# Layer 0's probabilities times values for all key blocks of a group in one piece, and the output weights' last split ahead of the first gated sum

## The chip, the cores and the metric

The kernel runs on one core of one Trainium2 chip. The core has five engines that each take their instructions in the order in which the program holds them: TensorE (PE, matmuls; PEld is its weight load), VectorE (DVE), ScalarE (ACT), GpSimd (POOL), and SyncE (SP), which here issues the DMAs. An engine whose next instruction waits for another engine or for a DMA stands still, and everything behind that instruction stands with it. The metric is the device time of one execution in microseconds (us). Before the change three runs gave a median of 1699.66 us (1698.5 to 1700.81).

## What is computed

Two layers of a diffusion backbone over 512 latent tokens and 256 context tokens of width 1024. Layer 0 mixes tokens by windowed attention with 16 query heads and 2 key/value heads of 64 and a sink logit per head; layer 1 by differential attention. Each layer goes on with a squared-ReLU MLP of width 4096. Sums pass through LayerNorm with DeepNorm scaling and gates from a conditioning vector. All is in float32.

```python
def block_fn(args):                       # layer 0, for each block of 128 queries
    s_lat = jnp.where(valid, einsum('bqhgd,bkhd->bhgqk', qblk, kblk) * scale, NEG_INF)
    s_ctx = einsum('bqhgd,bchd->bhgqc', qblk, kc) * scale
    p = softmax_with_sink(jnp.concatenate([s_lat, s_ctx], axis=-1), sink_f)
    o = einsum('bhgqk,bkhd->bqhgd', p[..., :3 * BLOCK], vblk)
    return o + einsum('bhgqc,bchd->bqhgd', p[..., 3 * BLOCK:], vc)
...
x = layer_norm(alpha * x + g1 * ax, ln1_g[i], ln1_b[i])     # ax = attention output @ wo
fx = sqrelu_mlp(x * (1.0 + sc2) + sh2, mlp_w1[i], mlp_w2[i])
x = layer_norm(alpha * x + g2 * fx, ln2_g[i], ln2_b[i])
```

## The kernel before

Tokens stand in six blocks of 128 (`tb`): four latent, two context. A weight of 128x1024 is loaded by DMA to `w_raw`, rounded by ACT to `w_h` (L264) and its remainder taken by DVE as `w_l` (L260); a product is then three matmuls, `w_h` times both parts of the tokens and `w_l` times one (`mm3`, L318 to L320). `wsplit` makes such a weight. Three raw buffers and four pairs of split buffers go round.

**What sets the order.** PE's order is fixed when the program is built. Generator jobs yield the conditions under which they can go on; a planner (`Flow`) keeps an estimated clock for every engine, and at each point lets the job of the smallest priority number go on whose condition holds. It knows a price per instruction by its size, and none for what stands next to it. For the other engines a scheduler orders the instructions by its own estimates, within dependences that the kernel can add by hand (`tc.add_manual_dep` with `ORDER`: the first instruction is to stand behind the second in the queue, without a semaphore).

**Layer 0's attention** works in 24 groups, each one block of queries and four heads (`group`). Groups of the four latent query blocks see 4 or 5 key blocks (two, or two or three, latent ones beside two of context), and the eight groups of the context blocks see 2. For each of the four heads PE makes the scores `s_ps` (two slots), DVE takes mask and minimum (`nm`), ACT the exponential `e` with its sum, DVE the reciprocal, POOL the product. Then for each key block `i` four transposes on PE put the probabilities of the four heads side by side in `pT_ps`; ACT (even `i`) or DVE (odd `i`) copies them to a buffer `pT`; and `av` multiplies them by the values `vv` into `o_ps`, two matmuls (128 rows by 64 columns of the array: even heads to the upper 64 partitions of the output, odd heads to the lower). `pend` is the list of the blocks that are copied and not multiplied yet, `pS` counts the `pT` buffers, four of them. `av` runs for two blocks as soon as both copies are due, or for the last one alone.

Jobs of larger priority numbers fill in: the query projection `q_ps`, then the streamed modulation weights (`ada_ps`, 12 pieces of eight matmuls that use 32 columns of the array each, and `ada_t`, their transposes), and from the end of those on the first half of the output projection (`out_proj`: `y_ps` with weights `a_wo`, six matmuls a piece). The projection of a token block can start once all four groups of that block are done.

**Layer 1's output projection** begins before its attention ends: for seven of the eight products of a token block and a half of the columns, three of the four weights (`u` = 0 to 2) are multiplied early (`out1`). The fourth weight of the second half (`st2["W1"]`) is split in `mlp1`'s first lines; `main1` then finishes the products in the order (half 0, block 0), (half 1, block 0), (half 0, block 1) and so on, and `gated_add` multiplies each with the gate (`g_tmp`) and adds it to `acc`; `stats` follows, then the LayerNorm.

Of the kernel before, what the change touches and what calls it, by code (L numbers as in the profile page):

```python
# [19 lines left out]
P = 128  # L20
D = 1024
# [195 lines left out]
def pool2(n):  # L217
    return n * 0.0022 + 0.12
# [16 lines left out]
def hybrid_block(ctx: ExitStack, tc: tile.TileContext, t: dict, out: bass.AP):  # L235
# [23 lines left out]
    def dv(n, deps, fn, lat=LAT, **kw):  # L259
        fn(**kw)  # L260
        return fl.op("D", dve(n), deps, lat)
# [5 lines left out]
    def gp(us, deps, fn, lat=LAT, **kw):  # L267
        fn(**kw)  # L268
        return fl.op("G", us, deps, lat)
# [29 lines left out]
    def wsplit(src, n=1024, raw=None, hl=None, pool=False):  # L299
        if raw is None:  # L300
            raw = raw_tile()
        if hl is None:
            hl = [wpool.tile([P, 1024], F32R, name="w_" + x, tag="w" + x, bufs=NH) for x in "hl"] + [rwh.get(), rwh]
        raw, rg, rr = raw
        h, l, hg, hr = hl
        q = dma(n, [rg], out=raw[:, :n], in_=src)
        a = ac(n, [q, hg], nc.scalar.copy, out=h[:, :n], in_=raw[:, :n])
        kw = dict(out=l[:, :n], in0=raw[:, :n], in1=f(h)[:, :n], op=ALU.subtract)
        d = gp(pool2(n), [a], nc.gpsimd.tensor_tensor, **kw) if pool else dv(n, [a], nc.vector.tensor_tensor, **kw)
        d.ring = rr  # L310
        rel = Task()
        rel.ring = hr
        return Weight(h, l, d, rel)
# [242 lines left out]
    def gated_add(pool, give, acc, half, pt, p, gate, last, scale=1.0):  # L556
        cs_ = slice(half * 512, (half + 1) * 512)
        tm = pool.tile([P, 512], F32, name="g_tmp", tag="tmp", bufs=2)
        m = dv(512, [p], nc.vector.tensor_tensor, out=tm, in0=pt, in1=gate[:, cs_], op=ALU.mult)
        give(m)  # L560
        if scale != 1.0:
            return dv(512, [m], nc.vector.scalar_tensor_tensor, out=acc[:, cs_], in0=acc[:, cs_], scalar=scale, in1=tm,
                      op0=ALU.mult, op1=ALU.add)
        if last:
            return dv(512, [m], nc.vector.tensor_tensor, out=acc[:, cs_], in0=acc[:, cs_], in1=tm, op=ALU.add)
        return gp(pool2(512), [m], nc.gpsimd.tensor_tensor, out=acc[:, cs_], in0=acc[:, cs_], in1=tm, op=ALU.add)
# [170 lines left out]
    with tc.tile_pool(name="qpool", bufs=6, side="right") as qpool, \  # L737
# [219 lines left out]

        oT = hx
        eS = Slots(fl, EB)
        pS = Slots(fl, 4)  # L960

        def etile(i):
            if i < EB:
# [3 lines left out]
        def group(n, tb, qd):  # L967
# [61 lines left out]


            def av_ok():
                return (len(pend) > 1 or len(pend) == 1 and i == len(kbs)) and fl.ok([x[3] for x in pend[:2]])


            i = 0
            while i < len(kbs) or pend:
                yield lambda: (YES if (i < len(kbs) and fl.ok([sm_.ok, pS.ok])) or av_ok() else NO)
                if i < len(kbs) and fl.ok([sm_.ok, pS.ok]) and len(pend) < 4:
                    pp = psm("pT_ps")
                    slot = sm_.take()  # L1040
                    for c, j in enumerate((0, 2, 1, 3)):
                        nc.tensor.transpose(out=pp[:, c * P:(c + 1) * P], in_=es[j][:, i * P:(i + 1) * P],  # L1042
                                            identity=ident)
                    p = fl.pe(4 * mm(128))
                    pt_ = pool.tile([P, 512], F32, name="pT", tag="pT", bufs=4)
                    xi = pS.take()
                    r = (dv(512, [p], nc.vector.tensor_copy, lat=XLAT, out=pt_, in_=pp) if i % 2 else
                         ac(512, [p], nc.scalar.copy, lat=XLAT, out=pt_, in_=pp))
                    sm_.give(slot, r)
                    if i == len(kbs) - 1:  # L1050
                        for q_ in esl:
                            eS.give(q_, p)
                    pend.append((i, kbs[i], pt_, r, xi))
                    i += 1
                else:
                    for _ in range(min(2, len(pend))):
                        p = av(*pend.pop(0))
            st0["done"] += 1
            if st0["done"] % 4 == 0:
# [468 lines left out]
    with tc.tile_pool(name="mlp1", bufs=1, reuse_waits="tile") as pool:  # L1528
        xraw["pool"] = pool
        hl = [late.tile([P, 1024], F32R, name="w_" + x, tag="w" + x, bufs=1) for x in "hl"]  # L1530
        acc = [pool.tile([P, D], F32, name="acc1", tag="acc", bufs=NXB) for _ in range(NXB)]
        for tb in range(NXB):
            dma(D, [], out=acc[tb], in_=x_res[tb])
        gx = bcast_load(pool, gate_d[(1, 2)][0:1], "g1x")
        queue["behind"] = queue["last"]
        st2["W1"].append(wsplit(t["b_wo"][1, 3], hl=hl + [None, None]))
        lb = bcast_load(pool, lnrow[1, 1:2], "l1b")
        scale_inplace(lb, ALPHA)
        A, B = affine(1, 0, 1, 1, 3, 4, "m1", 1)
        hx = hx_big("hx1m", SEQ)  # L1540
        ready = [NO] * NXB

        def done3(tb, st, r):
            fl.add(ln_job(pool, acc[tb], tb, hx, A, B, ready, st, r), 0)

        def done4(tb, st, r):
            if tb == 0:
                st2["g"] = bcast_load(pool, lnrow[1, 2:3], "l2g")
                st2["b"] = bcast_load(pool, lnrow[1, 3:4], "l2b")
            mv, rstd, d = moments(st, r)  # L1550
            cols = [slice(0, D)] if tb < NXB - 1 else [slice(0, 512), slice(512, D)]
            for c in cols:
                dv(c.stop - c.start, [r], nc.vector.scalar_tensor_tensor, out=acc[tb][:, c], in0=acc[tb][:, c],
                   scalar=mv[:, 0:1], in1=st2["g"][:, c], op0=ALU.subtract, op1=ALU.mult)
            for c in cols:
                dv(c.stop - c.start, [d], nc.vector.scalar_tensor_tensor, out=acc[tb][:, c], in0=acc[tb][:, c],
                   scalar=rstd, in1=st2["b"][:, c], op0=ALU.mult, op1=ALU.add)
                nc.sync.dma_start(out=out[tb * P:(tb + 1) * P, c], in_=acc[tb][:, c])

        def g2b():  # L1560
            yield
            return [bcast_load(pool, gate_d[(1, 5)][0:1], "g2x")]

        def main1():
            yield from tok_product(pool, oT, {0: st2["W"], 1: st2["W1"]}, [(h_, tb) for tb in range(NXB) for h_ in range(2)],
                                   acc, (gx,), done3, pre=st2["po"], late=(0, 1))
            queue["behind"] = None
            reload(gx, lnrow[1, 0:1])
            scale_inplace(gx, ALPHA)
            res = [lambda tb=tb: residual(acc[tb], gx, lb, last["pe"]) for tb in range(NXB)]  # L1570
            yield from mlp(1, hx, ready, apool, pool, SEQ, acc, g2b, done4, None, res)

        fl.add(main1(), 2)
        fl.run()
# [71 lines left out]
```

## Time and profile before

| | |
|---|---|
| median of three runs | 1699.66 us (1698.5 to 1700.81) |
| the profiled execution | 1701.68 us, its span 1699.9 us, mean granted clock 0.988 |
| layer 0's attention, scores to last group | about 70 to 323 us of the span |
| layer 1's output projection | about 1280 to 1327 us |

The page gives busy times by engine, the chain of work that ended last, and groups of instructions; the trace behind it gives single rows. A row of the timeline holds the start in us from the span's start, how long it took from its first instruction's start to its last one's end, the engine, line, operation, `out<-in`, the form, how many instructions are merged in it, and in square brackets how long the engine stood idle ahead of it and what ended that. Matmuls overlap, so their price is read from one start to the next. A product of plain float32 appears as two records, so `av` of one block as four. A stretch shows busy times of all engines between two points; its clock (1.00, or 0.50 in a few stretches) is what the throttle granted PE.

### The profile page before, as it was taken

The numbers are of one execution on the slowest core, as the hardware profiler recorded it, in microseconds if no ns is written. First come the engines' busy times: TensorE is split into PE (matmuls) and PEld (weight loads), VectorE is DVE, ScalarE is ACT, GpSimd is POOL, SyncE is SP. The second block draws the span as 40 slices with busy tenths as digits, with TensorE's granted clock in tenths as the row PEclk, the third lists the DMA queues.
The fourth block names the chain that finished last, engine by engine and source line by source line (L and its number), as shares of the span: only waits on it lengthen the run. The fifth ranks groups of instructions, "written<-read, shape, count | busy, mean of one in ns | idle before, by whom it ended". The sixth has DMA issues, their size and how long they took to land.

```text
span 1699.9 us, 23452 instructions
## 1 busy us (share of the span) xinstructions
PE 1626.4 (96%) x9129; PEld 1394.2 (82%) x9129; DVE 955.2 (56%) x1811; ACT 657.8 (39%) x1281; POOL 346.6 (20%) x314
## 2 busy tenths in 40 slices
PE   6899899999999999999999999999989799999998
PEld 4787567789879989979978998999877788888886
DVE  3665677676855444444446777677655553233436
ACT  3455565362223213202316555555542533222230
POOL 1234444200001101243220223221100001103422
PEclk9999999999999999999999999999899899999999
DMA  9110343343535334334323122211132323132321
GB/s 363 41 50 8 125 153 109 127 152 108 166 116 168 113 124 136 112 111 137 99 66 112 50 69 67 69 44 38 47 111 100 103 73 134 63 124 75 111 87 50
DMA packets 57240, 174.78 MB, mean 103 GB/s; under 512 B 7144, under 2 KB 13096, under 8 KB 57128
## 3 DMA queue, kind: packets, MB, share of 16 engines
q1 hardware_dynamic: 57128, 173.27, 30.6%
q8 instruction: 72, 1.18, 0.3%
q14 instruction: 40, 0.33, 0.1%
HBM read 165.35 MB, written 7.90 MB: 102 GB/s over the span
## 4 chain that ended last, share of the span: by engine, by line
PE 75%; DVE 10%; issue 5%; ACT 5%; DMA 3%; POOL 3%; SPq 0%; DVEq 0%; POOLq 0%; ACTq 0%
PE y_ps L320 10%; PE y_ps L319 10%; PE y_ps L318 10%; PE h_ps L318 8%; PE h_ps L319 8%; PE h_ps L320 8%; PE qkv_ps L318 2%; PE qkv_ps L319 2%; PE qkv_ps L320 2%; PE s_ps L1340 2%; PE o_ps L1024 2%; DVE w_l L260 2%; DVE e L260 2%; PE pT_ps L1042 2%; PE o_ps L1378 1%
## 5 line engine op out<-in xcount | busy, mean ns | idle before, releaser
L264 ACT CAST w_h<-w_raw 128x1024 fp32r<-128x1024 f32 (+1 forms) x185 | 186.4, 1015 | 414.6 <-PE y_ps L320 210.9
L260 DVE TENSOR_TENSOR w_l<-w_raw,w_h 128x1024 fp32r<-128x1024 f32 (+1 forms) x185 | 221.8, 1210 | 220.1 <-ACT w_h L264 219.2
L319 PE MATMUL y_ps<-w_l,hid 128*128 128x512 f32 x640 | 253.0, 395 | 1.8 <-DVE w_l L260 1.7
L320 PE MATMUL y_ps<-w_h,hid 128*128 128x512 f32 x640 | 253.0, 395 | 0.4 <-DVE hid L260 0.2
L318 PE MATMUL y_ps<-w_h,hid 128*128 128x512 f32 x640 | 253.1, 395 | 0.0
L268 POOL TENSOR_TENSOR relu<-relu 128x768 f32<-128x768 f32 (+1 forms) x48 | 80.7, 1681 | 609.4 <-ACT relu L264 609.4
L320 PE MATMUL h_ps<-hx0m,w_l 128*128 128x384 f32 (+1 forms) x528 | 176.2, 334 | 1.6 <-DVE w_l L260 1.6
L318 PE MATMUL h_ps<-hx0m,w_h 128*128 128x384 f32 (+1 forms) x528 | 176.3, 334 | 0.2 <-ACT w_h L264 0.2
L319 PE MATMUL h_ps<-hx0m,w_h 128*128 128x384 f32 (+1 forms) x528 | 175.8, 333 | 0.0
L319 PEld LDWEIGHTS y_ps<-w_l,hid 128*128 128x128 f32 x640 | 120.4, 188 | 31.3 <-DVE w_l L260 3.1
L320 PEld LDWEIGHTS y_ps<-w_h,hid 128*128 128x128 f32 x640 | 120.3, 188 | 30.0 <-DVE hid L260 1.6
L318 PEld LDWEIGHTS y_ps<-w_h,hid 128*128 128x128 f32 x640 | 120.4, 188 | 28.4
L318 PE MATMUL qkv_ps<-w_h,hx 128*128 128x384 f32 (+1 forms) x384 | 127.8, 333 | 0.1
L319 PE MATMUL qkv_ps<-w_l,hx 128*128 128x384 f32 (+1 forms) x384 | 123.3, 321 | 0.8 <-DVE w_l L260 0.8
L320 PE MATMUL qkv_ps<-w_h,hx 128*128 128x384 f32 (+1 forms) x384 | 123.2, 321 | 0.0
L268 POOL TENSOR_TENSOR e<-e,sm 128x512 f32<-128x512 f32 (+2 forms) x96 | 94.3, 998 | 120.4 <-DVE sm L260 79.8
L318 PE MATMUL h_ps<-hx1m,w_h 128*128 128x512 f32 (+1 forms) x288 | 107.8, 374 | 3.5 <-ACT relu L264 3.5
L319 PE MATMUL h_ps<-hx1m,w_h 128*128 128x512 f32 (+1 forms) x288 | 107.4, 373 | 0.0
L320 PE MATMUL h_ps<-hx1m,w_l 128*128 128x512 f32 (+1 forms) x288 | 107.3, 373 | 0.0
L320 PEld LDWEIGHTS h_ps<-hx0m,w_l 128*128 128x128 f32 x528 | 99.6, 189 | 2.9 <-DVE w_l L260 2.9
L318 PEld LDWEIGHTS h_ps<-hx0m,w_h 128*128 128x128 f32 x528 | 99.7, 189 | 0.8 <-ACT w_h L264 0.6
L319 PEld LDWEIGHTS h_ps<-hx0m,w_h 128*128 128x128 f32 x528 | 99.7, 189 | 0.1
(225 smaller groups left out, 3118.3 us busy)
## 6 DMA issues: line engine op xcount, KB each, us to landing
w_raw<-in_w SPq DMA_DIRECT2D x128, 512.0 KB, 3.5
w_raw<-in_w_adaT SPq DMA_DIRECT2D x56, 512.0 KB, 3.5
w_raw<-in_w_ada SPq DMA_DIRECT2D x24, 512.0 KB, 4.3
w_raw<-in_b_w SPq DMA_DIRECT2D x32, 384.0 KB, 3.2
raw<-in_w_ada SPq DMA_DIRECT2D x16, 512.0 KB, 9.7
w_raw<-in_a_wq SPq DMA_DIRECT2D x8, 512.0 KB, 4.4
w_raw<-in_a_wo SPq DMA_DIRECT2D x8, 512.0 KB, 4.3
w_raw<-in_b_wo SPq DMA_DIRECT2D x8, 512.0 KB, 3.6
```

The source lines that it names most:

```text
L260: fn(**kw)
L264: fn(**kw)
L268: fn(**kw)
L318: nc.tensor.matmul(out=o, lhsT=lh, rhs=rh, start=start, stop=False)
L319: nc.tensor.matmul(out=o, lhsT=lh, rhs=rl, start=False, stop=False)
L320: last["pe"] = nc.tensor.matmul(out=o, lhsT=ll, rhs=rh, start=False, stop=stop)
L1024: nc.tensor.matmul(out=po[odd * HD:odd * HD + HD, 0:256], lhsT=vv[:, kb, kvh], rhs=pt_[:, odd * 256:odd * 256 + 256], start=(i == 0), stop ...
L1042: nc.tensor.transpose(out=pp[:, c * P:(c + 1) * P], in_=es[j][:, i * P:(i + 1) * P], identity=ident)
L1340: nc.tensor.matmul(out=sp[:, c * 512:c * 512 + 384], lhsT=qTt[:, tt, hl, qb * P:(qb + 1) * P], rhs=kS[:, tt, c * 384:c * 384 + 384], start ...
L1378: nc.tensor.matmul(out=po[:, qp * 256:(qp + 1) * 256], lhsT=vt[:, kb, vl], rhs=pt_[:, pl, a * 256:a * 256 + 256], start=(kp == 0 and pl == ...
```

## The change

Three edits. In `group` there are six `pT` buffers in place of four, and `av` runs only when all blocks of the group are transposed and copied, or when no buffer is left; then for all that are pending. In `wsplit` the DVE's subtraction is kept by name, and `gated_add` orders its first multiplication behind the one that `mlp1` names: the split of the output weights' last part. No instruction is added or removed.

```diff
@@ wsplit
-        d = gp(pool2(n), [a], nc.gpsimd.tensor_tensor, **kw) if pool else dv(n, [a], nc.vector.tensor_tensor, **kw)
+        if pool:
+            d = gp(pool2(n), [a], nc.gpsimd.tensor_tensor, **kw)
+        else:
+            last["split"] = nc.vector.tensor_tensor(**kw)
+            d = fl.op("D", dve(n), [a])
@@ gated_add
-        m = dv(512, [p], nc.vector.tensor_tensor, out=tm, in0=pt, in1=gate[:, cs_], op=ALU.mult)
+        i = nc.vector.tensor_tensor(out=tm, in0=pt, in1=gate[:, cs_], op=ALU.mult)
+        if queue.get("split"):
+            tc.add_manual_dep(i.ins, queue.pop("split"), ORDER, reason="queue order")
+        m = fl.op("D", dve(512), [p])
@@ layer 0, group
-        pS = Slots(fl, 4)
+        pS = Slots(fl, 6)
...
-                return (len(pend) > 1 or len(pend) == 1 and i == len(kbs)) and fl.ok([x[3] for x in pend[:2]])
+                return pend and (i == len(kbs) or not fl.ok(pS.ok)) and fl.ok([x[3] for x in pend])
...
-                if i < len(kbs) and fl.ok([sm_.ok, pS.ok]) and len(pend) < 4:
+                if i < len(kbs) and fl.ok([sm_.ok, pS.ok]):
...
-                    pt_ = pool.tile([P, 512], F32, name="pT", tag="pT", bufs=4)
+                    pt_ = pool.tile([P, 512], F32, name="pT", tag="pT", bufs=6)
...
-                    for _ in range(min(2, len(pend))):
+                    for _ in range(len(pend)):
                         p = av(*pend.pop(0))
@@ mlp1
         st2["W1"].append(wsplit(t["b_wo"][1, 3], hl=hl + [None, None]))
+        queue["split"] = last["split"].ins.name
```

Three places of the order follow; the lines' numbers shift by up to eight. On PE, the sixth group (five key blocks) before, from its first `av` (`o_ps`, x4 is two blocks) on; `e_1488`, `e_1527`, `e_1508` and `e_1607` are its four heads' probabilities:

```order
L1024 MATMUL o_ps<-pT,v_118 64x256 x4
L1042 MATMUL pT_ps<-identr,e_1488 128x128
L1042 MATMUL pT_ps<-identr,e_1527 128x128
L1042 MATMUL pT_ps<-identr,e_1508 128x128
L1042 MATMUL pT_ps<-identr,e_1607 128x128
L1024 MATMUL o_ps<-pT,v_118 64x256 x4
L987 MATMUL s_ps<-kT_117,qT_1307 128x384 x2
L991 MATMUL s_ps<-kT_117,qT_1307 128x256 x2
L1024 MATMUL o_ps<-pT,v_118 64x256 x2
```

The same group after the change, from the transposes of its last key block on:

```order
L1049 MATMUL pT_ps<-identr,e_1545 128x128
L1049 MATMUL pT_ps<-identr,e_1583 128x128
L1049 MATMUL pT_ps<-identr,e_1564 128x128
L1049 MATMUL pT_ps<-identr,e_1662 128x128
L364 MATMUL ada_ps<-w_raw,cs 32x256 x8
L994 MATMUL s_ps<-kT_117,qT_1292 128x384 x2
L998 MATMUL s_ps<-kT_117,qT_1292 128x256 x2
L994 MATMUL s_ps<-kT_117,qT_1292 128x384 x2
L998 MATMUL s_ps<-kT_117,qT_1292 128x256 x2
L1031 MATMUL o_ps<-pT,v_118 64x256 x10
L388 MATMUL ada_t<-identr,ada_rows 128x128 x2
```

Three pieces of two, two and one blocks became one of five, and an `ada_ps` piece and two heads' scores of a later group stand between the last transposes and it. On PE, the end of the stage before: the last head's scores, and what stands ahead of the last group's transposes (after these rows come two more of `y_ps` and then the transposes):

```order
L991 MATMUL s_ps<-kT_117,qT_1841 128x256 x2
L318 MATMUL y_ps<-w_h,hx_92 128x512
L319 MATMUL y_ps<-w_l,hx_92 128x512
L320 MATMUL y_ps<-w_h,hx_92 128x512
L318 MATMUL y_ps<-w_h,hx_92 128x512
L319 MATMUL y_ps<-w_l,hx_92 128x512
L320 MATMUL y_ps<-w_h,hx_92 128x512
L1024 MATMUL o_ps<-pT,v_118 64x256 x4
L318 MATMUL y_ps<-w_h,hx_93 128x512
L319 MATMUL y_ps<-w_l,hx_93 128x512
L320 MATMUL y_ps<-w_h,hx_93 128x512
L318 MATMUL y_ps<-w_h,hx_93 128x512
```

The same place after the change; `e_3625` is the head whose scores stand in the first row:

```order
L998 MATMUL s_ps<-kT_117,qT_1791 128x256 x2
L1031 MATMUL o_ps<-pT,v_118 64x256 x4
L1049 MATMUL pT_ps<-identr,e_3551 128x128
L1049 MATMUL pT_ps<-identr,e_3585 128x128
L1049 MATMUL pT_ps<-identr,e_3574 128x128
L1049 MATMUL pT_ps<-identr,e_3625 128x128
```

Behind them come the second block's four transposes and the group's `av`. The `y_ps` pieces that stood here now stand earlier in the stage: the first one comes after the `av` of 11 groups, where it came in the midst of the fifteenth group's before. On DVE, at layer 1's output projection before:

```order
L260 TENSOR_TENSOR oT_8245<-oraw,oT_8245 128x512 x2
L260 TENSOR_TENSOR g_tmp<-y_ps,g1x 128x512
L260 TENSOR_TENSOR acc_12405<-acc_12405,g_tmp 128x512
L260 BN_STATS bn<-acc_12405 128x6
L260 TENSOR_TENSOR w_l<-w_raw,w_h 128x1024
L260 TENSOR_SCALAR l1b<-l1b 128x1024
L260 TENSOR_TENSOR g_tmp<-y_ps,g1x 128x512
```

And after the change:

```order
L260 TENSOR_TENSOR oT_8245<-oraw,oT_8245 128x512 x2
L312 TENSOR_TENSOR w_l<-w_raw,w_h 128x1024
L260 TENSOR_SCALAR l1b<-l1b 128x1024
L563 TENSOR_TENSOR g_tmp<-y_ps,g1x 128x512
L260 TENSOR_TENSOR acc_12405<-acc_12405,g_tmp 128x512
L260 BN_STATS bn<-acc_12405 128x6
L563 TENSOR_TENSOR g_tmp<-y_ps,g1x 128x512
```

The split moved ahead of the first gated sum, and the scaling of `l1b` with it; nothing else on DVE moved there. SP's queue holds the same DMAs; in layer 0 the loads of the modulation weights and of `a_wo` stand earlier in the program, and two small loads of the gate (`g1h`) stand ahead of the last modulation weight and the first of `a_wo`, where they stood behind the first of `a_wo`.

## The prediction

> **What bounds the kernel now.** I read the page first (busy shares, then the chain that ended last), then the stretches of the layer-0 attention, then who TensorE (PE) waits for in them.
>
> ```profile
> span 1699.9 us, 23452 instructions
> ...
> PE 1626.4 (96%) x9129; PEld 1394.2 (82%) x9129; DVE 955.2 (56%) x1811; ACT 657.8 (39%) x1281; POOL 346.6 (20%) x314
> ...
> PE 75%; DVE 10%; issue 5%; ACT 5%; DMA 3%; POOL 3%; SPq 0%; DVEq 0%; POOLq 0%; ACTq 0%
> ```
>
> PE is busy 96% of the span and holds 75% of the chain, so time is won in two ways only: PE does its work in less time, or one of its waits goes. The stretches (from:to, length, then busy us of PE, PEld, DVE, ACT, POOL, then clock, DMA share, GB/s) say the same of the attention:
>
> ```profile
> 180.00:260.00 80.00, 71.96 (x623) 49.29 (x624) 53.80 (x178) 44.73 (x106) 36.82 (x32) 1.00 0.47 152
> 325.00:345.00 20.00, 20.00 (x88) 16.10 (x87) 12.53 (x19) 3.17 (x4) 1.11 (x2) 1.00 0.85 288
> ```
>
> In the attention (first row) no other engine is full, and DMA is at 0.47; in the output projection behind it (second row) PE has no gap at all. PE's waits between 100 and 330 us (total, times, longest):
>
> ```profile
> PE s_ps L987 <- DVE nm L260: 3.6, 6, 2.2
> PE o_ps L1024 <- ACT pT L264: 2.2, 2, 1.4
> PE ada_t L384 <- ACT ada_rows L264: 1.6, 1, 1.6
> PE ada_ps L360 <- DMA w_raw<-in_w_ada: 1.1, 1, 1.1
> PE o_ps L1024 <- DVE pT L260: 0.6, 1, 0.6
> ```
>
> **Part 1: the AV matmuls in one pack.** Nothing is computed that was not computed before: 88 key blocks (16 latent groups of 4 or 5, eight context groups of 2), four AV records each. The order makes 47 packs of AV matmuls before and 24 after. What one pack costs beside its blocks is read from packs of one, two and three blocks (x4, x8, x12):
>
> ```profile
> 159.13 0.65 PE L1024 MATMUL o_ps<-pT,v 128*64 128x256 f32 x4
> 159.71 0.62 PE L987 MATMUL s_ps<-kT,qT 128*128 128x384 f32 x2
> ...
> 226.99 1.52 PE L1024 MATMUL o_ps<-pT,v 128*64 128x256 f32 x12
> 228.43 1.07 PE L360 MATMUL ada_ps<-w_raw,cs 128*32 128x256 f32 x16
> ...
> 279.76 0.39 PE L319 MATMUL y_ps<-w_l,hx 128*128 128x512 f32 x1
> 279.99 0.39 PE L320 MATMUL y_ps<-w_h,hx 128*128 128x512 f32 x1
> 280.31 1.08 PE L1024 MATMUL o_ps<-pT,v 128*64 128x256 f32 x8
> 281.33 0.74 PE L991 MATMUL s_ps<-kT,qT 128*128 128x256 f32 x4
> ```
>
> From start to the next row's start they take 0.58, 1.02 and 1.44 us: 0.43 us a block and 0.15 fixed. The pack also starts 0.32 us after the y_ps row ahead of it, where y_ps rows follow each other after 0.23: 0.09 more. So a pack costs 0.24 us beside its work, wherever the array goes from 128*128 to 128*64 and back. 23 packs fewer: 23 x 0.24 = 5.5 us. Eight times before, and once after, a pack stands next to an ada_ps row (128*32), which starts a pack of its own kind; there the two share one change, 7 x 0.09 = 0.6 us that is lost. Net **-4.9 us** of PE work in a stretch where PE is the bound.
>
> **The waits of that stretch.** The order is drawn anew, so each wait is looked up in it.
>
> The 2.8 us of o_ps waiting for its pT copies (ACT 2.2, DVE 0.6): before, a pack began as soon as two copies were due. Now at least one pair of score matmuls, and mostly an ada_ps or y_ps piece, stands between a five-block group's last transposes and its pack, and the last block is asked for 4 x 0.43 = 1.7 us into the pack. Bounds 0 and -2.8; I take **-2.7**. The two ada waits (1.6 and 1.1): now the pack of 2.3 us stands between an ada_ps piece and its ada_t, and ada_ps pieces are 3.5 us apart or more. Bounds 0 and -2.7; I take **-2.4**. The other s_ps waits (3.6 less 2.2, 1.4 us) stay, and grow because PE comes 5 us earlier to a DVE that has the same work: between 0 and as much again; **+0.7**.
>
> The longest wait, 2.18 us, has a cause of its own (chain row, DVE row, PE row, two stretches, and the loads' median time to landing):
>
> ```profile
> 249.90 6.18 DMA w_raw<-in_a_wo
> ...
> 257.18 1.23 DVE L260 TENSOR_TENSOR w_l<-w_raw,w_h 128x1024 fp32r<-128x1024 f32 x1 [2.49 <-ACT w_h L264]
> ...
> 259.46 0.51 PE L987 MATMUL s_ps<-kT,qT 128*128 128x256 f32 x2 [2.18 <-DVE nm L260]
> ...
> 256.85:260.26 3.41, 1.23 (x10) 0.99 (x9) 3.08 (x10) 1.17 (x4) 0.00 (x0) 1.00 0.84 282
> 260.26:263.67 3.41, 3.41 (x18) 3.19 (x18) 2.42 (x9) 3.41 (x8) 1.36 (x2) 0.50 0.34 136
> ...
> w_raw<-in_a_wo SPq DMA_DIRECT2D x8, 512.0 KB, 4.3
> ```
>
> The first output weights land 6.18 us after their issue, ACT and DVE stand in order behind them, and PE's scores behind DVE. Right behind it PE runs 3.41 us at half clock: 1.7 us lost. After the change these four splits come some 16 us of PE work earlier, and the first to ask for the late ones is y_ps itself: from the release of the second load PE has 6.2 us of rows until it needs that weight's low part. Load, cast and split take 4.3 to 6.2 (median and longest load) + 1.05 + 1.23 = 6.6 to 8.5 us, so PE waits 0.4 to 2.3 us. Two gate loads that ran beside the slow load are now issued ahead of the last w_ada load, so I take the short side, 0.8: **-1.4**, and half of the clock loss: **-0.85**.
>
> **What is late next: the end of the stage.** Because the output projection starts earlier, its y_ps rows are used up before the last group. There the order has: last score matmul, a pack of two blocks, the group's transposes, its pack, nothing between. How long a head's chain is, shows at the same place before:
>
> ```profile
> 314.58 0.48 PE L991 MATMUL s_ps<-kT,qT 128*128 128x256 f32 x2
> 315.62 0.47 DVE L260 CUSTOM_DVE_ANT_0 e<-s_ps,mask,nsink 128x256 f32<-128x256 f32 x1
> 316.57 0.51 ACT L264 ACTIVATE e<-e,nm 128x257 f32<-128x257 f32 x1 [0.57 <-DVE e L260]
> 317.44 0.61 POOL L268 TENSOR_TENSOR e<-e,sm 128x256 f32<-128x256 f32 x1 [0.41 <-DVE sm L260]
> 318.89 1.03 PE L1042 MATMUL pT_ps<-identr,e 128*128 128x128 f32 x8
> 319.52 0.59 ACT L264 COPY pT<-pT_ps 128x512 f32<-128x512 f32 x1 [1.64 <-PE pT_ps L1042]
> 319.96 0.69 DVE L260 COPY pT<-pT_ps 128x512 f32<-128x512 f32 x1 [1.62 <-PE pT_ps L1042]
> ```
>
> From the scores' end (315.06) to POOL's end (318.05) 3.0 us. The last group's fourth transpose has only a pack of two (1.1) and three transposes (0.35) to hide it: 1.6 us idle. Its copies end 1.22 and 1.76 us after the first transpose, where PE's eight take 0.87: about 0.55 more. **+2.2 us**. Bounds 0 (a chain half as long) and 3.0.
>
> The clock may add to that. The row above shows that a stretch of 3.41 us with PE at work for 1.23 was followed by one at half clock, and the tail has 2.2 us of waits and 1.7 of transposes close together: another 1.7 us, at even odds **+0.85**. [...]
>
> Layer 0 together: -4.9 - 2.7 - 2.4 + 0.7 - 1.4 - 0.85 + 2.2 + 0.85 = **-8.5 us**. Behind it PE is busy 20.00 of 20 us (325:345 above), so what is won there is kept.
>
> **Part 2: the last split ahead of the first gated sum.**
>
> ```profile
> 1290.95 1.04 ACT L264 CAST w_h<-w_raw 128x1024 fp32r<-128x1024 f32 x1
> ...
> 1299.41 0.69 DVE L260 TENSOR_TENSOR g_tmp<-y_ps,g1x 128x512 f32<-128x512 f32 x1 [7.63 <-PE y_ps L320]
> ...
> 1301.46 1.21 DVE L260 TENSOR_TENSOR w_l<-w_raw,w_h 128x1024 fp32r<-128x1024 f32 x1
> 1302.59 0.69 DVE L260 TENSOR_SCALAR l1b<-l1b 128x1024 f32<-128x1024 f32 x1
> ...
> 1302.73 0.50 PE L319 MATMUL y_ps<-w_l,oT 128*128 128x512 f32 x1 [3.13 <-DVE w_l L260]
> 1304.18 0.69 DVE L260 TENSOR_TENSOR g_tmp<-y_ps,g1x 128x512 f32<-128x512 f32 x1 [0.91 <-PE y_ps L320]
> ...
> 1304.18:1322.63 18.45, 15.49 (x78) 12.40 (x76) 18.23 (x37) 9.35 (x20) 1.64 (x3) 0.98 0.29 112
> ...
> 1283.52 0.43 SPq L275 DMA_DIRECT2D l1b<-in_lnrow  x1
> DMA to landing us min/median/max: 5.0/5.0/5.0
> ```
>
> The split's input is ready at 1291.99, and DVE idles 7.63 us until the first y_ps is done. Put ahead, it runs from 1292.0 to 1293.2 in that idle time, and the scaling of l1b (landed by 1288.5), which moves with it, to 1293.9. The added order has g_tmp wait for an instruction that ended 5 us earlier: nothing. PE's wait of 3.13 us goes. The next limit is DVE: it is busy 18.23 of the following 18.45 us. Its second g_tmp moves from 1304.18 to the end of the first sum's statistics at 1301.46; PE, resuming at 1299.6, has that product by 1301.1. **-2.7 us**, bounds -2.2 and -3.13. The raw buffer comes free 9 us earlier and its next load with it; the cast behind that load waits for PE, so nothing collides.
>
> **The sum.** -8.5 - 2.7 = -11.2 us against the profiled execution's 1701.68: 1690.5. That execution lies 2.0 us over the median of the three runs; against 1699.66 the sum gives 1688.5. A redrawn order also has small waits that I did not find; what I did not list before (0.2 to 0.4 us each) suggests some 1.5 us. Forecast: **1690.0 us**.
>
> **The rivals.**
> - *The tail and the weights eat layer 0's gain.* If y_ps waits 2.3 us for its weights and halves the clock as before, the tail halves it too (+1.7), the ada waits only move and half of the o_ps waits stays, layer 0 is at -4.9 - 1.4 + 0.1 + 0.7 + 2.2 + 1.7 = -1.6, with part 2 at -4.3, with the small waits at -2.8: 1696.9, inside 0.2%. For it: both places stand in the order. Against: it needs each bound at its bad end. 0.15.
> - *Slower: half clock in the groups.* [...] 0.05.
> - *Part 2 gives nothing*, if the first sum was to wait anyway: 1692.7. DVE's 7.63 idle us speak against it. 0.08.
> - That the packs don't form is excluded by the order: 24, one a group.
>
> **How the numbers follow.** Forecast 0.72. Half-clock windows elsewhere can come or go as the work shifts, 1.7 us each; two fewer and an open tail at 0 give 1684.5, the first rival 1697: the range. A measurement here tells about 0.2% (3.4 us) from no change; faster by more 0.82 (forecast, most of the third rival and a part of the first), within 0.14, slower 0.04.
>
> **What would show it.** Right: PE's o_ps packs in 24 pieces with 0.24 us saved a pack; no o_ps wait over 0.5 us before the last group; PE idle near 1.6 us ahead of the last transposes; no y_ps wait of 3.13 us, DVE's gap ahead of g_tmp at about 5.7 us. Wrong: a wait over 3 us in the attention that before has not, or half-clock stretches in it.

## The result and the profile after

| | before | after |
|---|---|---|
| median of 7 runs each | 1698.5 us (1692.58 to 1700.81) | 1685.71 us (1683.57 to 1690.51) |
| ratio, 95% interval | | 0.9938 (0.9921 to 0.9955) |
| the profiled execution, its span | 1701.68 us, 1699.9 us | 1690.51 us, 1688.7 us |
| layer 0's first transposes to the next stage's first, on PE | 244.01 us | 238.15 us |

The change makes the kernel faster by 0.45 to 0.79%. The ratio is taken over all executions and is not the quotient of the two medians, which is 0.9925. One execution of a run reported below, the kernel before with later copies, took 1799.99 us at a granted clock of 0.846, where its other seven had 0.988 to 0.993, and is left out of that row. The three lines of the page after that answer to those of before:

```profile
span 1688.7 us, 23443 instructions
...
PE 1617.0 (96%) x9129; PEld 1392.0 (82%) x9129; DVE 956.7 (57%) x1811; ACT 658.2 (39%) x1281; POOL 344.4 (20%) x314
...
PE 74%; DVE 10%; issue 5%; ACT 4%; DMA 3%; POOL 3%; SPq 0%; POOLq 0%; DVEq 0%; ACTq 0%
```

PE executes the same 9129 records, 9.4 us less busy time; shares and chain look the same. Where the time went shows only by stretch. The stage of the table, before and after (from:to, length, then busy us of PE, PEld, DVE, ACT, POOL, then clock, DMA share, GB/s):

```profile
102.09:346.10 244.01, 234.57 (x1608) 174.95 (x1607) 164.34 (x513) 120.50 (x285) 94.32 (x96) 0.99 0.31 100
```

```profile
101.61:339.76 238.15, 228.22 (x1609) 175.11 (x1608) 163.35 (x512) 120.97 (x285) 94.10 (x96) 0.99 0.31 102
```

PE is busy 234.57 - 228.22 = 6.35 us less in it, while its idle time (length less busy) goes from 9.44 to 9.93. So the whole gain of the first part is in PE's work and none is in its waits, although the waits are different ones. PE's waits after, between 100 and 330 us (total, times, longest):

```profile
PE pT_ps L1049 <- ACT pT L264: 2.9, 4, 0.9
PE pT_ps L1049 <- POOL e L268: 2.2, 1, 2.2
PE y_ps L323 <- DVE w_l L312: 1.5, 2, 1.3
PE ada_t L388 <- ACT ada_rows L264: 1.4, 2, 0.8
PE o_ps L1031 <- DVE pT L260: 0.9, 2, 0.6
PE ada_ps L364 <- DMA w_raw<-in_w_ada: 0.6, 1, 0.6
PE o_ps L1031 <- ACT pT L264: 0.2, 1, 0.2
PE s_ps L994 <- DVE nm L260: 0.2, 1, 0.2
```

The s_ps waits of 3.6 us are down to 0.2, the o_ps waits from 2.8 to 1.1; in their place transposes wait (pT_ps, 5.1 us). What the largest group of these is, the records around one of them show (start, length, engine, line, operation, and in brackets the idle time before it):

```profile
189.28 1.26 PE L1049 MATMUL pT_ps<-identr,e 128*128 128x128 f32 x10
...
190.93 0.67 DVE L260 COPY pT<-pT_ps 128x512 f32<-128x512 f32 x1
190.97 0.83 ACT L264 ACTIVATE e<-e,nm 128x641 f32<-128x641 f32 x1
...
191.80 1.06 ACT L264 COPY pT<-pT_ps 128x512 f32<-128x512 f32 x2
...
192.42 1.09 PE L1049 MATMUL pT_ps<-identr,e 128*128 128x128 f32 x8 [0.86 <-ACT pT L264]
```

Before, a pack stood behind every two blocks' transposes. Now a group's four or five blocks are transposed close together, PE gets ahead of the engines that copy the results out of PSUM (ACT's copies stand behind its 0.83 us exponential), and waits for the next free PSUM tile.

The second part, on DVE in layer 1's output projection after the change:

```profile
1283.77 1.22 DVE L312 TENSOR_TENSOR w_l<-w_raw,w_h 128x1024 fp32r<-128x1024 f32 x1 [0.26 <-ACT w_h L264]
1284.91 0.69 DVE L260 TENSOR_SCALAR l1b<-l1b 128x1024 f32<-128x1024 f32 x1
1291.14 0.69 DVE L563 TENSOR_TENSOR g_tmp<-y_ps,g1x 128x512 f32<-128x512 f32 x1 [5.55 <-PE y_ps L324]
```

The split and the scaling of l1b stand ahead of the first g_tmp, in what was idle time; 5.55 us of it are left. PE has no y_ps wait there any more. Of the 3.13 us some 0.3 come back: the next xn_t waits 1.0 us for ACT instead of 0.7. Against before, PE's matmuls are 8.24 us earlier ahead of this place (1250 us of before) and 11.09 us earlier behind it (1326 us): 2.85 us.

### The profile page after: what moved, and what is told of

It reads as the page before. It is cut to its first block, busy times and chain, and to the rows that moved or that the text cites. A ratio compares the mean times of both kernels' runs of the same rounds, so it can differ in the third digit from the quotient of the medians.

```text
span 1688.7 us, 23443 instructions
## 1 busy us (share of the span) xinstructions
PE 1617.0 (96%) x9129; PEld 1392.0 (82%) x9129; DVE 956.7 (57%) x1811; ACT 658.2 (39%) x1281; POOL 344.4 (20%) x314
## 4 chain that ended last, share of the span: by engine, by line
PE 74%; DVE 10%; issue 5%; ACT 4%; DMA 3%; POOL 3%; SPq 0%; POOLq 0%; DVEq 0%; ACTq 0%
PE y_ps L324 10%; PE y_ps L323 10%; PE y_ps L322 10%; PE h_ps L322 8%; PE h_ps L323 8%; PE h_ps L324 8%; PE o_ps L1031 2%; PE qkv_ps L322 2%; PE qkv_ps L323 2%; PE s_ps L1347 2%; PE qkv_ps L324 2%; DVE w_l L312 2%; PE pT_ps L1049 2%; DVE e L260 1%; PE o_ps L1385 1%
```

## The experiments

Eleven more kernels were run. "Stage" is the stretch of the table above; a ratio is to the kernel before, timed on the same chip beside it. The experiments ran on two chips, so across rows it is the ratios that compare, not the medians.

| run | median us | ratio (95%) | packs | stage us | of it PE busy |
|---|---|---|---|---|---|
| before | 1698.5 | 1 | 47 | 244.0 | 234.6 |
| after | 1685.71 | 0.9938 (0.9921 to 0.9955) | 24 | 238.2 | 228.2 |
| part 1 only | 1692.33 | 0.9964 (0.995 to 0.9978) | 24 | 236.5 | 226.7 |
| part 2 only | 1693.64 | 0.9978 (0.9966 to 0.9989) | 47 | 242.9 | 234.5 |
| zero matmuls between all blocks | 1715.82 | 1.0103 (1.0086 to 1.012) | 88 | 265.6 | 259.7 |
| as many, together | 1705.22 | 1.0044 (1.0028 to 1.006) | 48 | 255.2 | 247.8 |
| four buffers, new rule | 1696.99 | 1.0001 (0.9987 to 1.0014) | 32 | 247.9 | 235.3 |
| six buffers, old rule | 1695.62 | 0.999 (0.9978 to 1.0002) | 37 | 246.0 | 234.2 |
| output product held back | 1687.07 | 0.9938 (0.9921 to 0.9955) | 24 | 236.5 | 227.3 |
| copies planned 0.7 us later | 1682.65 | 0.9918 (0.9902 to 0.9935) | 24 | 233.4 | 227.2 |
| kernel before, copies 0.7 us later | 1703.03 | 1.003 (1.0018 to 1.0041) | 42 | 249.1 | 236.5 |
| copies 0.7 us later and product held back | 1682.07 | 0.9909 (0.9896 to 0.9922) | 24 | 232.2 | 226.1 |
| copies 1.0 us later | 1688.92 | 0.9953 (0.9941 to 0.9965) | 24 | 237.4 | 227.7 |

**Each part alone.** Part 1 only:

```diff
-        queue["split"] = last["split"].ins.name
```

> The change without its second part: the last split of the output weights stands behind the first gated product again. Theory (the two parts add up, the first is worth about 8 us by the starting time of the second layer's first matmuls, the second 2.85 us by the shift between 1256 and 1324 us): 2.85 us slower than the changed kernel, about 8 us faster than the one before, and the wait of 3.13 us ahead of y_ps near 1317 us is back. Rival (the split only trades one wait for another): within 1 us of the changed kernel.

Part 2 only (the buffers of the tile `pT` go back to four as well):

```diff
-        pS = Slots(fl, 6)
+        pS = Slots(fl, 4)
...
-                return pend and (i == len(kbs) or not fl.ok(pS.ok)) and fl.ok([x[3] for x in pend])
+                return (len(pend) > 1 or len(pend) == 1 and i == len(kbs)) and fl.ok([x[3] for x in pend[:2]])
...
-                if i < len(kbs) and fl.ok([sm_.ok, pS.ok]):
+                if i < len(kbs) and fl.ok([sm_.ok, pS.ok]) and len(pend) < 4:
...
-                    for _ in range(len(pend)):
+                    for _ in range(min(2, len(pend))):
```

> The change without its first part: four buffers, two key blocks in a row, 47 packs. Theory: 2.85 us faster than the kernel before (ratio 0.9983), with no y_ps wait over 2 us near 1317 us, and about 8 us slower than the changed kernel, because 23 packs more are entered and left. Rival (the first part gains nothing of its own, and the 8 us are a half-clock window that happened to fall elsewhere): within 3 us of the changed kernel.

By the ratios part 1 is worth 6.1 us (3.7 to 8.5) and part 2 3.7 us (1.9 to 5.8), together 9.8, and both at once 10.5. Part 1 comes out below the 8 us expected, whose figure came from two single executions, though its interval reaches them. Within these intervals the two add up, and the rivals (a split that only trades waits; a first part that gains nothing) are out: with part 1 alone the wait of 3.13 us is back at 1292, with part 2 alone it is gone and the stage's PE busy time is that of before (234.5 against 234.6).

**What a pack costs.** In both kernels a matmul of zeros over the whole width of the array is added into o_ps, 64 times: once behind every block but the last of each pack, or all of a pack's behind its first block. The first of the two, without the lines that make the tile `zz` of zeros:

```diff
-                    for _ in range(len(pend)):
+                    for c in range(len(pend), 0, -1):
                         p = av(*pend.pop(0))
+                        if c > 1:
+                            nc.tensor.matmul(out=po[:, 0:32], lhsT=zz, rhs=ident[:, 0:32], start=False, stop=False)
```

> The changed kernel with 64 small 128x128 matmuls of zeros (32 columns) added into o_ps, one between every two blocks of a pack, so that each pack of m blocks is cut into m pieces by a matmul over all 128 columns of the array. The values stay the same. Theory (a pack's price is that of going from 128x128 to 128x64 and back, 0.24 us by the prediction, 0.28 us by the PE's accounts of the two traces): against the run with the same 64 matmuls in 24 places, 40 more such changes, so 9.6 to 11.2 us longer in the stage, and each cut block starts about 0.28 us later than it does without. Rival (what a pack costs is a handover of the job or the copy that it waits for, not the form of the matmul): within 2 us of that run.

> The same 64 matmuls of zeros, all of a pack's behind its first block, so that the packs are cut in 24 places. Theory: the 24 cuts cost 24 x 0.24 to 0.28 = 5.8 to 6.7 us against the changed kernel, beside the 64 matmuls' own time (some 0.06 us each, 4 us, by the two-column-group pieces of like size), so about 10 us above it, and 9.6 to 11.2 us below the run that cuts 64 times. Rival: the same time as the run that cuts 64 times, within 2 us.

The same pack of four blocks in the changed kernel, with the zero matmuls together, and with them between (the first column is the start; what matters is from the first o_ps to the s_ps behind it; the last line is used further down):

```profile
104.41 1.95 PE L1031 MATMUL o_ps<-pT,v 128*64 128x256 f32 x16
106.28 0.62 PE L994 MATMUL s_ps<-kT,qT 128*128 128x384 f32 x2
```

```profile
104.53 0.65 PE L1033 MATMUL o_ps<-pT,v 128*64 128x256 f32 x4
105.11 0.85 PE L1070 MATMUL o_ps<-identr,zz 128*128 128x32 f32 x6
105.90 1.52 PE L1033 MATMUL o_ps<-pT,v 128*64 128x256 f32 x12
107.34 0.62 PE L996 MATMUL s_ps<-kT,qT 128*128 128x384 f32 x2
```

```profile
104.54 0.65 PE L1033 MATMUL o_ps<-pT,v 128*64 128x256 f32 x4
105.12 0.41 PE L1068 MATMUL o_ps<-identr,zz 128*128 128x32 f32 x2
105.46 0.65 PE L1033 MATMUL o_ps<-pT,v 128*64 128x256 f32 x4
106.04 0.41 PE L1068 MATMUL o_ps<-identr,zz 128*128 128x32 f32 x2
...
107.30 0.65 PE L1033 MATMUL o_ps<-pT,v 128*64 128x256 f32 x4
107.88 0.62 PE L996 MATMUL s_ps<-kT,qT 128*128 128x384 f32 x2
...
108.58 0.51 PE L996 MATMUL s_ps<-kT,qT 128*128 128x384 f32 x2
```

1.87 us, 2.81 us and 3.34 us. The last two do the same matmuls; two more cuts cost 0.53 us, 0.265 each. Over the whole kernel 40 more cuts cost 1715.82 - 1705.22 = 10.6 us, again 0.265 each; that the two figures agree so closely is in part chance, since in the stage PE is busy 12.0 us longer (1.6 of it for 3.41 us more of half clock) and waits 1.6 us less. The rival (a handover of the job, a copy that is waited for) would have made the two runs equal. So the price belongs to the switch between 128*128 and 128*64 and back, whoever asks for it. No run put zero matmuls of the 128*64 form between the blocks; that it is the form, and not any foreign matmul, rests on rows where the product changes and the form does not: in the run with zeros together a q_ps matmul follows a score matmul after 0.23 us (108.40 to 108.63), as q_ps matmuls follow each other (108.63 to 108.86). What the 0.265 us of a switch and back are spent on, the traces do not show. My estimate for the zero matmuls themselves was a miss: each is two records 0.11 us apart, 0.22 us and not 0.06, which puts both runs some 10 us higher than expected against the changed kernel. It is the same in both and leaves their difference alone.

**Buffers or rule.** Four buffers with the new rule (again with the tile's buffers), then six with the old one:

```diff
-        pS = Slots(fl, 6)
+        pS = Slots(fl, 4)
```

> The change with four buffers for the probabilities in place of six, and the new rule kept: 32 packs instead of 24 (the four groups of key blocks of each of two token blocks that have five need two). Theory (0.266 us a pack from the run with zero matmuls): PE busy in the first layer's attention 2.1 us above the changed kernel's. If a ring that runs full makes transposes wait for a pack to end, waits are added to that; if the four waits of pT_ps behind ACT's copies come from transposes that stand four or five in a row, they stay. Rival (buffers, not packs, gave the gain): PE busy equal to that of the kernel before, 6 us above the changed one.

```diff
-                return pend and (i == len(kbs) or not fl.ok(pS.ok)) and fl.ok([x[3] for x in pend])
+                return (len(pend) > 1 or len(pend) == 1 and i == len(kbs)) and fl.ok([x[3] for x in pend[:2]])
...
-                if i < len(kbs) and fl.ok([sm_.ok, pS.ok]):
+                if i < len(kbs) and fl.ok([sm_.ok, pS.ok]) and len(pend) < 6:
...
-                    for _ in range(len(pend)):
+                    for _ in range(min(2, len(pend))):
```

> Six buffers with the old rule (a pack as soon as two blocks lie ready): 37 packs. Theory: PE busy in the first layer's attention 13 x 0.266 = 3.5 us above the changed kernel's and 10 x 0.266 = 2.7 below that of the kernel before. Rival (the buffers alone gave the gain): PE busy within 1 us of the changed kernel's. The waits tell which of the two edits took away the s_ps waits of before (3.6 us) and brought the pT_ps waits of after (2.9 us beside the tail).

Neither half alone can be told from no change, so buffers alone are not the gain. And both kernels still hold part 2: held against part 2 alone (0.9978, stage 242.9 us) they are 3.9 and 2.0 us slower by the ratios, with intervals that overlap, and their stages are 5.1 and 3.1 us longer. So in these orders the first part gains only when rule and buffers come together. But the sizes were missed. With four buffers PE busy is 7.0 us above the changed kernel where the eight packs account for 2.1; up to 3.4 us more are half clock (10.24 us of the stage at 0.5 instead of 3.41), and the rest I could not separate. With six buffers and the old rule it is 0.4 us below before, not 2.7; why is open too. The waits are clearer. Four buffers, then six with pairs:

```profile
PE ada_ps L364 <- DMA w_raw<-in_w_ada: 3.5, 3, 2.0
PE ada_t L388 <- ACT ada_rows L264: 2.6, 5, 1.2
PE y_ps L323 <- DVE w_l L312: 2.2, 1, 2.2
```

```profile
PE ada_t L388 <- ACT ada_rows L264: 3.4, 2, 1.7
PE s_ps L998 <- DVE nm L260: 3.2, 1, 3.2
```

With four buffers the redrawn order meets the stream of the w_ada and a_wo weights at other places: 8.3 us of waits in the three rows, where the changed kernel has 3.5 (y_ps, ada_t, ada_ps). With pairs the long s_ps wait of before is still there (3.2) and no transpose waits behind ACT's pT copy. So the new rule removes the one and brings the other, though with four buffers it brings only 0.6 us of it.

**The tail.**

```diff
+            st0["scored"] = n + 1
             yield lambda: YES if (1, tb) in qmm else NO
...
+                if tb == 4:
+                    yield lambda: YES if st0["scored"] == 24 else NO
                 yield sm_.ok
                 pt = psm("y_ps")
```

> The changed kernel, with the output product of token block 4 (four pieces of 1.44 us) held back until the last group's scores have been issued, so that there is work for the PE ahead of the last transposes. Theory A (the last group's softmax on DVE, ACT and GpSimd sets when its probabilities are there, and the held pieces leave gaps of the same size where they stood): the wait of 2.17 us becomes less than 0.5, but waits of s_ps or pT_ps before it grow by as much, and the first xn_t of the next stage comes within 1 us of the changed kernel's. Theory B (the PE sets it: the held pieces delay the last scores): the last probabilities come 2 to 4 us earlier and the stage is 2 to 3 us shorter.

The wait of 2.17 us behind GpSimd is gone, and others have come:

```profile
PE s_ps L998 <- DVE nm L260: 1.0, 2, 0.7
PE o_ps L1032 <- ACT pT L264: 0.8, 1, 0.8
```

All idle time of the stage is 9.2 us against 9.9: theory A, the softmax sets the tail and a filler mostly moves the gap. The next stage begins 1.6 us earlier, not within 1, which is as much as costs the half-clock stretch that this run's stage lacks. Part 1 alone, whose stage has the changed kernel's order and no such stretch either, has the same length, 236.5 us; and the ratio is the changed kernel's, 0.9938.

That this stretch is no fixed price of the tail, two runs with the same order there show, the changed kernel and part 1 alone (part 2 acts 940 us later). The last transposes, the pack behind them and the first output matmul, and then the stretch of 313.37 to 316.79 with the one before it (clock in the third column from the end); after:

```profile
312.24 0.77 PE L1049 MATMUL pT_ps<-identr,e 128*128 128x128 f32 x5 [2.17 <-POOL e L268]
313.24 1.89 PE L1031 MATMUL o_ps<-pT,v 128*64 128x256 f32 x8 [0.24 <-ACT pT L264]
315.06 0.80 PE L322 MATMUL y_ps<-w_h,hx 128*128 128x512 f32 x1
```

```profile
309.96:313.37 3.41, 1.00 (x9) 0.66 (x9) 0.98 (x4) 1.24 (x4) 0.61 (x1) 1.00 0.26 76
313.37:316.79 3.42, 3.42 (x12) 1.95 (x13) 0.79 (x2) 0.38 (x1) 0.00 (x0) 0.50 0.00 0
```

And part 1 alone, the same rows, the stretch of 313.37 to 316.79, and two cells of its own grid, which is explained behind them:

```profile
312.39 0.77 PE L1049 MATMUL pT_ps<-identr,e 128*128 128x128 f32 x5 [2.16 <-POOL e L268]
313.40 1.20 PE L1031 MATMUL o_ps<-pT,v 128*64 128x256 f32 x8 [0.24 <-ACT pT L264]
314.52 0.50 PE L322 MATMUL y_ps<-w_h,hx 128*128 128x512 f32 x1
```

```profile
313.37:316.79 3.42, 3.39 (x18) 2.26 (x19) 0.94 (x2) 0.95 (x2) 0.00 (x0) 1.00 0.00 0
...
307.66:311.07 3.41, 2.23 (x15) 0.94 (x13) 2.87 (x10) 1.06 (x3) 1.55 (x2) 1.00 0.48 142
311.07:314.48 3.41, 1.85 (x13) 0.92 (x13) 0.85 (x2) 0.90 (x3) 0.61 (x1) 1.00 0.03 11
```

The same gap, 2.17 and 2.16 us, at nearly the same time, and once the clock is halved for 3.4 us and once not. What goes with that can be read from the traces. Within each of the 13 traces (before, after and the eleven experiments) all half-clock stretches begin whole multiples of 3.413 us apart (before at 260.26, then 33, 235, 275, 293, 311 and 420 multiples later; in the changed kernel at 313.37, then 217, 258, 275, 292 and 402), so the stretches of an execution lie on a grid, and the profiled executions differ in where it lies. Half clock goes with how little PE was busy in the one cell of the grid before: of all full-clock cells from 60 us on, the 42 with PE busy for less than 1.5 us were all followed by half clock, of some 6000 with more than 1.75 us only six were, and between the two both happened. In the traces of before and after alone it was nine of nine under 1.5 us, four of eight between, and none of 919 above. In the changed kernel the whole gap lies in one cell, with PE busy for 1.00 us; with part 1 alone the grid lies so that the gap falls on two, with 2.23 and 1.85 us.

**The transposes that wait for a copy.** The planner is told that a copy is seen 0.7 us after its end, not 0.2:

```diff
-                    r = (dv(512, [p], nc.vector.tensor_copy, lat=XLAT, out=pt_, in_=pp) if i % 2 else
-                         ac(512, [p], nc.scalar.copy, lat=XLAT, out=pt_, in_=pp))
+                    r = (dv(512, [p], nc.vector.tensor_copy, lat=0.7, out=pt_, in_=pp) if i % 2 else
+                         ac(512, [p], nc.scalar.copy, lat=0.7, out=pt_, in_=pp))
```

> The changed kernel, with the planner told that a copy of transposed probabilities out of PSUM is seen 0.7 us after its end, not 0.2. Theory (the four waits of pT_ps behind ACT's copies, 2.9 us, come from transposes that the planner sends before the copies are out of PSUM): these waits fall below 1 us, other work stands in their place, still 24 packs, and the stage is about 2 us shorter. Rival (there is no other work ready at those places): the waits change their name, and the stage keeps its length within 1 us.

The same number in the kernel before:

> The kernel before with only the planner's number for the copies changed, 0.7 us in place of 0.2; 42 packs instead of 47. Theory (the late copies hurt because the changed rule sets a group's transposes close together; before, packs stood between them): no pT_ps wait to remove here, PE busy 5 x 0.266 = 1.3 us less by the packs, and the time within 2 us of that less, about 1696. Rival (the number was wrong in both kernels and is worth the same in both): about 3 us or more below the kernel before in time, and 4 to 5 us shorter in the stage.

The second dose, `lat=1.0`:

> The changed kernel with copies seen 1.0 us after their end, as the second dose. Theory (the copy's own 0.59 to 0.68 us are in the plan already, and 0.7 covers the wait): no pT_ps wait behind ACT's copies is left to remove, so within 1.5 us of the run with 0.7, with longer gaps of s_ps as the transposes now stand too late. Rival (still early at 0.7): 1 to 2 us faster again.

In the changed kernel the waits behind ACT's copies fall from 2.9 to 0.2 us and the stage is 4.7 us shorter, more than expected. In time the gain over the changed kernel is not clear of the noise: 0.9918 against 0.9938, with intervals that overlap. Its waits:

```profile
PE pT_ps L1049 <- POOL e L268: 1.9, 3, 1.5
PE s_ps L998 <- DVE nm L260: 1.6, 2, 0.9
PE s_ps L994 <- DVE nm L260: 1.1, 1, 1.1
...
PE pT_ps L1049 <- ACT pT L264: 0.2, 1, 0.2
```

The y_ps wait of 1.5 and the ada_t waits of 1.4 are gone as well, in return for 2.5 us more of s_ps. In the kernel before the same edit makes it slower by 0.3% (0.18 to 0.41%), where I expected 1.3 us less: five packs fewer are there, but PE is busy 236.5 us and not less than 234.6 (two half-clock stretches of 3.41 us lie in the stage, one before), and it waits for the weights and for the split of a block's queries (`qstg`):

```profile
PE ada_ps L360 <- DMA w_raw<-in_w_ada: 5.5, 4, 1.9
PE qT_ps L920 <- DVE qstg L260: 1.9, 1, 1.9
```

So my figure was a miss, but the rival is out: the number is not worth the same in both; with the new rule it takes away the waits that the rule brought. At 1.0 us the pT_ps waits behind ACT's copies are as at 0.7 (0.2 us) and one s_ps wait of 5.2 us has come, 1688.92. Each number gave one redrawn order, so how much of these differences is the number's and how much the luck of the order is not shown.

**Both mends together.**

> The changed kernel with copies seen 0.7 us later and token block 4's output product held back until the last scores are out. Theory (the held product only moves the tail's wait; what it gains is the half-clock window of 1.6 us that follows a gap of 1.5 to 2 us): the wait of 1.49 us behind GpSimd's e goes, s_ps waits of 0.7 to 1.5 us come in its place, and no half-clock window lies near 309; the time is 0 to 1.7 us below that of the run with the later copies alone (1682.65). Rival (the two edits spoil each other in the planner's order): slower than that run by 1 us or more.

1682.07 us, 0.9909 (0.9896 to 0.9922): no pT_ps wait behind GpSimd is left, nor a half-clock stretch in the stage, and s_ps waits 5.0 us in all. That is faster than the kernel before; against the changed one the intervals just touch, and from the run with the later copies alone (0.9918) it can't be told apart.

## Why the prediction was right, and where it was not

Forecast 1690.0 us, faster; measured 1685.71, inside the range and 4.3 us below the forecast. The sum, -11.2 us against the profiled execution, is what the two profiled executions show, 1701.68 and 1690.51, but not by the same terms. The measured ones leave 0.3 us, which is itself a balance: between 378 and 1190 us of before PE loses 1.0 us again, and a half-clock stretch near 1199 is 6.83 us long in place of 10.24, which gives 1.4.

| term | predicted | measured |
|---|---|---|
| packs, net of the shared ada_ps change | -4.9 | -6.4 (PE busy of the stage) |
| waits of the stage (o_ps -2.7, ada -2.4, s_ps +0.7, weights -1.4, tail +2.2) | -3.6 | +0.5 |
| half clock in the stage | 0 (-0.85 and +0.85) | 0: one stretch of 3.41 us goes, one comes |
| part 2 | -2.7 | -2.85 |
| before the stage | - | -0.5 |
| a half-clock stretch behind the stage | - | about -1.6 |

- *The packs.* The mechanism held: 24 packs, and the price belongs to the switch. It was too small, 0.24 against 0.265 with zero matmuls: the step looked at the o_ps rows and the row behind them only up to its start, and the first matmuls behind a pack take longer as well. With real work behind the pack that is more than with zeros: score matmuls last 0.62 us behind a pack and 0.51 behind other scores (107.88 and 108.58 in the run with zeros between), 0.1 us on top of the 0.24. 23 x 0.265 less the change shared with ada_ps pieces is 5.5 us, 23 x 0.34 less the same 7.2 (an estimate, as if scores followed every pack). The measured 6.4 lie between, so the packs can account for all of it, but no run divides it.
- *The waits were mis-sized, by 4.1 us.* This is the step that failed. It looked up each wait of before in the new order and found most of them covered, but asked too little which new ones the order makes. The transposes behind ACT's copies (2.9 us) it did not list at all, though the order shows a group's four or five blocks transposed close together. The ada waits moved rather than went (1.9 us left, not 0.4). The s_ps waits were to grow by 0.7 and fell to 0.2 instead.
- *"No o_ps wait over 0.5 us before the last group"* was wrong once: 0.62 us at 294.
- *The weights.* y_ps waits 1.5 us, 0.8 predicted, within its 0.4 to 2.3. No clock loss follows it.
- *The tail.* 2.17 us idle ahead of the last transposes where 1.6 was predicted, and 0.57 around them where 0.55 was. The mechanism was as described, and the holding test shows that it is the softmax that ends last there.
- *The clock.* Even odds for a half-clock stretch in the tail was the right thing to say: it came in the changed kernel and not with part 1 alone, behind the same gap. The gap's length does not decide the case, since 2.17 us went with a half-clock stretch and 2.16 us without; what differs is where the gap lies on the grid. Half clock goes more closely with PE's busy time when the transposes are counted in it: with them left out, cells under 1.2 us were followed by half clock 39 times and 54 times not (ten and eight in the traces of before and after), where with them all 42 under 1.5 us were. Half clock in the groups, to which the prediction gave 0.05, did not come in the changed kernel: the one half-clock stretch of its stage is that of the tail, 313.37 to 316.79.
- *Part 2* went as worked out, 5.55 us of DVE's idle time being left where about 5.7 was predicted.
- The 1.5 us for small waits were meant for what I could not find. What I did not find was larger, and it was offset by the packs' price and by a half-clock stretch of before that the profile of after has not:

```profile
372.90:376.31 3.41, 3.41 (x19) 3.41 (x17) 1.64 (x5) 3.04 (x10) 0.00 (x0) 0.50 0.00 1
```

```profile
367.41:370.82 3.41, 3.41 (x32) 3.41 (x31) 0.90 (x4) 3.41 (x11) 0.00 (x0) 1.00 0.00 0
```

The first row is before, the second about the same place in the program after: 19 matmuls in 3.41 us against 32. Of the other runs some have such a stretch there and some don't, so it can't be booked to the change. That the sum came out to the tenth is luck, the more so as the profiled execution of after is the slowest of its seven.

## What to carry to other kernels

Count the switches of the array's form, not only the matmuls: a piece of 128*64 work between pieces of 128*128 work cost 0.265 us here beside its own, somewhat more in front of scores, and can be priced by cutting packs with matmuls that add zeros. When work is gathered into longer packs, look for what used to stand between the pieces: here the packs had given ACT time to empty PSUM (no transpose waited for its pT copies before, 2.9 us of it after), and the planner's number for those copies had to follow (0.7 us took the new waits away; with 1.0 the kernel was slower than with 0.7, and in the kernel before 0.7 did harm). And don't size an edit of an order by its direct price alone: the new rule with four buffers raised the waits of y_ps, ada_t and ada_ps from 3.5 to 8.3 us and left nothing of the first part's gain.

## What the runs showed of the hardware

- A switch from 128*128 to 128*64 and back cost 0.265 us beside the work, measured with zero matmuls between a pack's blocks against as many together: 40 more of them 10.6 us (1715.82 against 1705.22).
- In the 13 traces the clock was halved for 3.41 us or a multiple at a time (6.83 near 1194 in the changed kernel, 10.24 near 1199 in the one before), but for the last stretch of a trace, which the span's end cuts. The stretches of one execution lay on a grid of 3.413 us, and they followed cells in which PE was busy for less than about half the time (under 1.5 us in 42 of 42, over 1.75 us in six of some 6000). So the same gap in the same order, 2.17 us in the changed kernel and 2.16 with part 1 alone, went with a half-clock stretch in one execution and with none in the other, by where the grid lay.
- Such a stretch cost about 1.6 us where PE was full: 19 matmuls in it (372.9 before) against 32 at full clock (367.41 after), and PE's lead over the kernel before grows from 6.28 to 7.87 us across the one at 372.9. The spread of executions of one kernel goes with the mean clock only in part: of seven of the changed kernel the fastest, 1683.57 us, shows 0.994 and the slowest, 1690.51 us, 0.991, but so does one of 1685.71.
